# A gate matrix from one 256-column matmul a token, its two parts added on the way out of PSUM

## The chip, the cores and the metric

One core of a Trainium2 chip runs the whole program. The metric is the device time of one execution in microseconds (us); the median of several runs is compared. The profile comes from one execution of its own. Engines are named as the profile names them: PE is TensorE's matmul side and PEld its weight loads, DVE is VectorE, ACT is ScalarE, POOL is GpSimd, SP is SyncE, which issues most DMAs.

## What is computed

Two layers of a transformer-like backbone over 512 latent and 256 context tokens. Each layer ends in a PEER block: every token picks, for each of 8 heads, 16 of 16384 single-neuron experts by product keys, and sums gate times activation times value row. Cut to what matters here:

```python
best, ci = lax.top_k(cand, PEER_TOPK)            # 8 heads x 16 picks = 128 picks a token
i1 = take_along_axis(si[:, :, 0], ci // 16)      # first key index, 0..127
i2 = take_along_axis(si[:, :, 1], ci % 16)       # second key index, 0..127
expert = i1 * 128 + i2
gate = softmax(best)
act = gelu(einsum('td,thkd->thk', h, u[expert]))
out = einsum('thk,thkd->td', gate * act, v[expert])
```

For some 128-token tiles the kernel gathers the expert rows from HBM. For the others ("dense" tiles: all four latent tiles in layer 0, three in layer 1) it computes the activation of all 16384 experts and multiplies it by a matrix of gates that is zero outside the picks. That gate matrix is what the change touches.

## The kernel before

**The dense path.** The 16384 experts are 128 blocks `b` of 128. In the *scored* stage (`scored`, lines 1297 to 1325) each block's rows of u are loaded (`tab`, two blocks a DMA, from SP), cast to a high part on ACT (`uH`, line 1312), reduced to a low part on DVE (`uL`, line 1314), and multiplied with the tokens by 24 matmuls (`pa`, lines 133 to 135, 512 columns in layer 0, 384 in layer 1). ACT applies the gelu (`aw`, line 1318) and stores it to HBM, or keeps it in SBUF (`ar`) for the last blocks; a kept block is multiplied by its gates at once (line 1323). In the stage after it (`py`, lines 1348 to 1390) the stored activations are read back with the gates (`wt`, line 1360) and multiplied with the rows of v.

**The gates.** `gates` (lines 1202 to 1238) makes, for each token, the 128 x 128 matrix of gates over (i1, i2) by one-hots: with the picks on the partitions, `oh[:, 0]` is the one-hot of i1, `oh[:, 1]` that of i2 (both f16, from comparing `iota4` with the index, line 1226), and `og` (line 1229) is the first one-hot times the gate, twice: once with the f16 gate and once with what f16 rounding left of it. The product over the picks is a matmul. Four tokens go together (a *group*): two DVE instructions for the one-hots, one for `og`, 8 matmuls of 128 columns (line 1234: for each token the two parts accumulate in the same columns of PSUM), one ACT instruction (line 1235) that scales the four matrices and writes them into the tile `W`. The four tokens are the innermost, contiguous index of `oh` and `og`, so a matmul of one token reads its operands with a step of four f16 elements, 8 bytes, for the weights (`oh[:, 1, :, q]`) and for the moving columns alike. Eight groups fill `W` (2 MB), which a DMA from ACT's queue stores (line 1237). A tile has 32 groups: 128 in layer 0, 96 in layer 1, 224 in all, and 28 DMAs of `W`. `W` has one buffer; `pw` (PSUM), `oh` and `og` have two each.

**Order.** Every engine runs its own instructions in order. The order is made when the program is built, by a planner (`schedule_with_timeline_sim=True`, line 1562) that places instructions by priority and by durations of its own. `gated` is a generator: line 1338 draws its units between the blocks (a unit is the choice of the experts of a tile, or 8 groups), evenly over the first 19 (layer 0) or 15 (layer 1) sets of four blocks. When all are drawn, their SBUF is freed and used for kept activations (line 1344). Gathers for the other tiles run beside it: POOL issues them (line 1465), DVE takes the dot products and accumulates (lines 1476, 1483).

**PSUM.** The pool `pw` is opened at line 1295, before the scores (line 1328), with two buffers of one bank; the pools of the scores take three banks until they close, and `pa` and the modulation units have three.

Of the kernel before, what the change touches and what calls it, by code (L numbers as in the profile page):

```python
# [8 lines left out]
F32 = mybir.dt.float32  # L9
# [4 lines left out]
AF = mybir.ActivationFunctionType  # L14
OP = mybir.AluOpType
AX = mybir.AxisListType
PSUM = bass.MemoryType.PSUM

P = 128
# [10 lines left out]
GSCALE = 4096.0  # L30
# [36 lines left out]
class Kernel:  # L67
# [1134 lines left out]
    def gates(self, t, pk, pool, ps):  # L1202

        nc = self.nc
        pT = ps.tile([P, 3, P], F32, name="pT", tag="pw")
        for j in range(3):
            nc.tensor.transpose(pT[:, j], pk[:, j], self.ident)
        pkT = pool.tile([P, 3, P], F32, name="pkT")
        nc.scalar.copy(pkT, pT)

        gt = pool.tile([P, P], F32, name="gt")
        nc.vector.tensor_scalar(gt, pkT[:, 2], GSCALE, None, OP.mult)
        g2 = pool.tile([P, 2, P], F16, name="g2")
        nc.vector.tensor_copy(g2[:, 0], gt)
        nc.vector.tensor_tensor(g2[:, 1], gt, g2[:, 0], OP.subtract)
        ix = pool.tile([P, 2, P], F16, name="ix")
        nc.vector.tensor_copy(ix, pkT[:, 0:2])
        yield
        for s_ in range(4):
            W = pool.tile([P, P, 32], F32, name="W", bufs=1)  # L1220
            for t4 in range(8):
                tt = slice(s_ * 32 + t4 * 4, s_ * 32 + t4 * 4 + 4)

                oh = pool.tile([P, 2, P, 4], F16, name="oh")
                for z in range(2):
                    nc.vector.tensor_tensor(oh[:, z], self.iota4, ix[:, z, tt].unsqueeze(1).to_broadcast([P, P, 4]),  # L1226
                                            OP.is_equal)
                og = pool.tile([P, 2, P, 4], F16, name="og")
                nc.vector.tensor_tensor(og, oh[:, 0].unsqueeze(1).to_broadcast([P, 2, P, 4]),
                                        g2[:, :, tt].unsqueeze(2).to_broadcast([P, 2, P, 4]), OP.mult)  # L1230
                pw = ps.tile([P, 4, P], F32, name="pw")
                for q in range(4):
                    for z in range(2):
                        nc.tensor.matmul(pw[:, q], oh[:, 1, :, q], og[:, z, :, q], start=z == 0, stop=z == 1)  # L1234
                nc.scalar.activation(W[:, :, t4 * 4:t4 * 4 + 4], pw.rearrange("p q i -> p i q"), AF.Copy,  # L1235
                                     scale=1.0 / GSCALE)
            nc.scalar.dma_start(self.wscr[:, 4 * t + s_], W)
            yield

# [21 lines left out]
    def peer(self, l, st):  # L1261
        tc, nc, i = self.tc, self.nc, self.i
# [10 lines left out]
        with ExitStack() as sb:  # L1273
# [18 lines left out]
            if wc:  # L1292
                mu = (sb.enter_context(self.pool(name="mu", bufs=1)),
                      sb.enter_context(self.pool(name="psm", bufs=1, space=PSUM)))
            pw = sb.enter_context(self.pool(name="pw", bufs=2, space=PSUM))

            def scored(g, late=None):

# [27 lines left out]

            with ExitStack() as s2:
                self.scores(l, hH, hL, LAT, sv, sif, s2, gat.tick)
            if not wc:
                gat.pick(0, self.choose(3, sv, sif, sp, it), sp)  # L1330
            gp = sg.enter_context(self.pool(name="sg", bufs=2, side="right"))
# [235 lines left out]
```

## Time and profile before

| | |
|---|---|
| median of 3 runs | 4957.31 us (4954.19 to 4966.87) |
| the profiled execution | 4952.64 us; its span from first to last instruction 4950.8 us |
| PE busy | 4408.5 us, 89% of the span, 27525 matmuls |
| DVE busy | 3639.2 us, 74% |
| ACT busy | 1870.6 us, 38% |
| POOL busy | 1322.9 us, 27% |
| mean granted TensorE clock | 0.92 |

The page's first part gives busy time of each engine; its shares are averages over stages with different limits. So the stages with gates are read apart: layer 0 makes them from 1260 to 1880 us, layer 1 from 3760 to 4180 us. A window's row gives busy time and the number of instructions of each engine, the granted clock (1.00 is 2.4 GHz, 0.50 is 1.2 GHz), and what the DMA engines did. Matmuls are pipelined: the duration of one is longer than the distance to the next.

### The profile page before, as it was taken

The numbers are of one execution on the slowest core, as the hardware profiler recorded it, in microseconds if no ns is written. First come the engines' busy times: TensorE is split into PE (matmuls) and PEld (weight loads), VectorE is DVE, ScalarE is ACT, GpSimd is POOL, SyncE is SP. The second block draws the span as 40 slices with busy tenths as digits, with TensorE's granted clock in tenths as the row PEclk, the third lists the DMA queues.
The fourth block names the chain that finished last, engine by engine and source line by source line (L and its number), as shares of the span: only waits on it lengthen the run. The fifth ranks groups of instructions, "written<-read, shape, count | busy, mean of one in ns | idle before, by whom it ended". The sixth has DMA issues, their size and how long they took to land. (4 is left out here: it accounts for less than half of the span.)

```text
span 4950.8 us, 73840 instructions
## 1 busy us (share of the span) xinstructions
PE 4408.5 (89%) x27525; PEld 3651.6 (74%) x27525; DVE 3639.2 (74%) x7395; ACT 1870.6 (38%) x3349; POOL 1322.9 (27%) x1390
## 2 busy tenths in 40 slices
PE   7778797889999988999999887898898998999899
PEld 4567676677788777788777655876688897977787
DVE  3974666879976775788888787658489865779855
ACT  3533245433333333333333353345333333333333
POOL 0026641243211112332322133453123200223100
PEclk8778787899999989999999887888899998999999
DMA  7444655347887878999999644664428865899975
GB/s 270 151 115 115 180 164 173 108 162 280 291 312 272 326 274 302 354 333 368 366 353 356 215 131 107 172 189 129 141 77 306 327 226 189 309 338 355 349 220 182
DMA packets 544360, 1186.54 MB, mean 240 GB/s; under 512 B 62768, under 2 KB 342720, under 8 KB 491264
## 3 DMA queue, kind: packets, MB, share of 16 engines
q1 hardware_dynamic: 436624, 615.77, 37.8%
q0 software_dynamic: 72432, 460.62, 25.7%
q10 hardware_dynamic: 34944, 105.43, 5.6%
q8 instruction: 216, 3.54, 0.3%
q14 instruction: 144, 1.18, 0.1%
HBM read 1005.19 MB, written 176.50 MB: 239 GB/s over the span
## 5 line engine op out<-in xcount | busy, mean ns | idle before, releaser
L1465 POOL DMA_INDIRECT row<-in_uv,eidx x384 | 593.9, 1547 | 1529.4 <-DVE accc L1483 1125.7
L133 PE MATMUL pa<-hH,uH 128*128 128x512 f32 (+1 forms) x2048 | 760.7, 371 | 43.4 <-ACT aw L1318 28.1
L135 PE MATMUL pa<-hH,uL 128*128 128x512 f32 (+1 forms) x2048 | 760.0, 372 | 23.7 <-DVE uL L1314 23.5
L134 PE MATMUL pa<-hL,uH 128*128 128x512 f32 (+1 forms) x2048 | 753.8, 368 | 0.0
L134 PE MATMUL py<-vL,GH 128*128 128x512 f32 x1792 | 700.7, 393 | 11.8 <-DVE vL L1370 11.6
L135 PE MATMUL py<-vH,GL 128*128 128x512 f32 x1792 | 696.1, 390 | 0.0
L133 PE MATMUL py<-vH,GH 128*128 128x512 f32 x1792 | 589.8, 394 | 50.9 <-ACT vH L1368 41.9
L1476 DVE SCALAR_TENSOR_TENSOR row<-row,h2c 128x1024 f32<-128x1024 f32 x384 | 472.3, 1235 | 77.3 <-DMA row<-in_uv,eidx 76.6
L1483 DVE SCALAR_TENSOR_TENSOR accc<-row,dt,accc 128x1024 f32<-128x1024 f32 x384 | 497.7, 1296 | 36.8 <-ACT dt L1480 29.3
L1312 ACT CAST uH<-tab 128x1024 fp32r<-128x1024 f32 x256 | 268.7, 1050 | 657.9 <-PE pa L134 622.2
L133 PEld LDWEIGHTS pa<-hH,uH 128*128 128x128 f32 x2048 | 393.1, 192 | 92.6 <-ACT aw L1318 35.1
L135 PEld LDWEIGHTS pa<-hH,uL 128*128 128x128 f32 x2048 | 392.3, 192 | 80.3 <-DVE uL L1314 33.9
L133 PEld LDWEIGHTS py<-vH,GH 128*128 128x128 f32 x1792 | 336.4, 189 | 132.1 <-ACT vH L1368 53.3
L134 PEld LDWEIGHTS pa<-hL,uH 128*128 128x128 f32 x2048 | 392.4, 192 | 40.3 <-issue 0.4
L134 PEld LDWEIGHTS py<-vL,GH 128*128 128x128 f32 x1792 | 338.0, 189 | 95.3 <-DVE vL L1370 25.7
L1314 DVE TENSOR_TENSOR uL<-tab,uH 128x1024 fp32r<-128x1024 f32 x256 | 318.7, 1246 | 115.6 <-ACT uH L1312 115.3
L135 PEld LDWEIGHTS py<-vH,GL 128*128 128x128 f32 x1792 | 337.4, 188 | 69.8
L1370 DVE TENSOR_TENSOR vL<-tab,vH 128x1024 fp32r<-128x1024 f32 x256 | 308.6, 1220 | 18.2 <-ACT vH L1368 18.0
L1379 ACT CAST GH<-G 128x512 fp32r<-128x512 f32 (+1 forms) x180 | 102.9, 572 | 518.9 <-PE py L134 365.5
L1226 DVE TENSOR_TENSOR oh<-iota,ix 128x512 f16<-128x512 f16 x448 | 171.8, 423 | 144.1 <-PE pw L1234 144.0
L1234 PE MATMUL pw<-og,oh 128*128 128x128 f16 x1792 | 238.1, 297 | 41.8 <-ACT W L1235 25.3
L1368 ACT CAST vH<-tab 128x1024 fp32r<-128x1024 f32 x256 | 261.0, 1044 | 23.1 <-DMA tab<-in_uv 23.1
(382 smaller groups left out, 8595.5 us busy)
## 6 DMA issues: line engine op xcount, KB each, us to landing
tab<-in_uT SPq DMA_DIRECT2D x128, 1024.0 KB
tab<-in_uv SPq DMA_DIRECT2D x128, 1024.0 KB
wscr<-W ACTq DMA_DIRECT2D x28, 2048.0 KB
wmod<-in_w_mod SPq DMA_DIRECT2D x48, 512.0 KB
row<-in_wq SPq DMA_DIRECT2D x24, 1024.0 KB
ascr<-aw ACTq DMA_DIRECT2D x96, 256.0 KB
row<-in_w_mod POOLq DMA_DIRECT2D x24, 1024.0 KB
av<-ascr SPq DMA_DIRECT2D x48, 512.0 KB
```

Of the source, the lines that this page charges most:

```text
L133: mm(out, lh, rh, start=first, stop=False)
L134: mm(out, lh, rl, start=False, stop=False)
L135: mm(out, ll, rh, start=False, stop=last)
L1226: nc.vector.tensor_tensor(oh[:, z], self.iota4, ix[:, z, tt].unsqueeze(1).to_broadcast([P, P, 4]), OP.is_equal)
L1234: nc.tensor.matmul(pw[:, q], oh[:, 1, :, q], og[:, z, :, q], start=z == 0, stop=z == 1)
L1312: nc.scalar.copy(uH, ur)
L1314: nc.vector.tensor_tensor(uL, ur, uH.bitcast(F32), OP.subtract)
L1368: nc.scalar.copy(vH, vr)
L1370: nc.vector.tensor_tensor(vL, vr, vH.bitcast(F32), OP.subtract)
L1465: self.K.nc.gpsimd.indirect_dma_start(out=r, out_offset=None, in_=self.K.i[f"uv{self.l}"], in_offset=bass.IndirectOffsetOnAxis(ap=self.idx ...
L1476: nc.vector.scalar_tensor_tensor(rows[z][:, 0:D], rows[z][:, 0:D], 1.0, self.h[:, a], OP.mult, OP.mult, accum_out=dt[:, z:z + 1])
L1483: nc.vector.scalar_tensor_tensor(acc, v, dt[:, z:z + 1], acc, OP.mult, OP.add)
```

## The change

For each group of four tokens: the two one-hots are made by one DVE instruction; the two parts of `og` are read as one moving operand of 256 columns, so that a token has one matmul (4 a group, not 8) and its two parts land side by side in PSUM; ACT scales the first part into `W` as before, and a new DVE instruction adds the second part, scaled, to what ACT wrote. `pw` doubles to two banks a buffer, and its pool is opened after the scores.

```diff
-                for z in range(2):
-                    nc.vector.tensor_tensor(oh[:, z], self.iota4, ix[:, z, tt].unsqueeze(1).to_broadcast([P, P, 4]),
-                                            OP.is_equal)
+                nc.vector.tensor_tensor(oh, self.iota4.unsqueeze(1).to_broadcast([P, 2, P, 4]),
+                                        ix[:, :, tt].unsqueeze(2).to_broadcast([P, 2, P, 4]), OP.is_equal)
...
-                pw = ps.tile([P, 4, P], F32, name="pw")
+                pw = ps.tile([P, 4, 2, P], F32, name="pw")
                 for q in range(4):
-                    for z in range(2):
-                        nc.tensor.matmul(pw[:, q], oh[:, 1, :, q], og[:, z, :, q], start=z == 0, stop=z == 1)
-                nc.scalar.activation(W[:, :, t4 * 4:t4 * 4 + 4], pw.rearrange("p q i -> p i q"), AF.Copy,
-                                     scale=1.0 / GSCALE)
+                    nc.tensor.matmul(pw[:, q], oh[:, 1, :, q], og[:, :, :, q], start=True, stop=True)
+                w4 = W[:, :, t4 * 4:t4 * 4 + 4]
+                nc.scalar.activation(w4, pw[:, :, 0].rearrange("p q i -> p i q"), AF.Copy, scale=1.0 / GSCALE)
+                nc.vector.scalar_tensor_tensor(w4, pw[:, :, 1].rearrange("p q i -> p i q"), 1.0 / GSCALE, w4, OP.mult,
+                                               OP.add)
             nc.scalar.dma_start(self.wscr[:, 4 * t + s_], W)
...
-            pw = sb.enter_context(self.pool(name="pw", bufs=2, space=PSUM))
...
                 self.scores(l, hH, hL, LAT, sv, sif, s2, gat.tick)
+            pw = sb.enter_context(self.pool(name="pw", bufs=2, space=PSUM))
```

## Rows read from the trace of the kernel before

**Rows 1.** The page's first part: busy us, share of the span, instructions.
```profile
PE 4408.5 (89%) x27525; PEld 3651.6 (74%) x27525; DVE 3639.2 (74%) x7395; ACT 1870.6 (38%) x3349; POOL 1322.9 (27%) x1390
```
**Rows 2.** Windows: length, busy PE, PEld, DVE, ACT, POOL (instructions), clock, DMA.
```profile
1260.00:1440.00 180.00, 177.91 (x909) 142.99 (x908) 159.37 (x341) 67.30 (x117) 40.53 (x27) 0.98 0.84 304
1440.00:1830.00 390.00, 381.86 (x2067) 309.44 (x2065) 278.25 (x448) 142.47 (x259) 67.72 (x51) 0.99 0.81 298
3640.00:3780.00 140.00, 129.46 (x708) 123.41 (x707) 134.11 (x521) 55.12 (x85) 28.00 (x32) 0.98 0.58 209
3780.00:4000.00 220.00, 195.97 (x1164) 184.83 (x1164) 190.35 (x314) 85.78 (x163) 63.97 (x32) 0.95 0.85 312
4000.00:4150.00 150.00, 145.86 (x937) 140.96 (x937) 87.67 (x153) 59.08 (x91) 0.00 (x0) 0.99 0.55 194
```
**Rows 3.** Windows of tile pw alone: length, busy PE, ACT (instructions), clock, DMA.
```profile
1260.00:1440.00 180.00, 27.27 (x208) 14.36 (x25) 0.98 0.84 304
1440.00:1830.00 390.00, 88.52 (x672) 49.61 (x86) 0.99 0.81 298
1830.00:1882.00 52.00, 19.63 (x144) 11.01 (x19) 0.54 0.45 170
3780.00:4000.00 220.00, 45.41 (x336) 24.48 (x42) 0.95 0.85 312
4000.00:4150.00 150.00, 42.04 (x320) 22.49 (x39) 0.99 0.55 194
4150.00:4178.00 28.00, 15.23 (x112) 9.36 (x16) 0.50 0.34 138
```
**Rows 4.** Groups by line: count, busy us, mean ns, idle before and its releaser.
```profile
L1226 DVE TENSOR_TENSOR oh<-iota,ix 128x512 f16<-128x512 f16 x448 | 171.8, 423 | 144.1 <-PE pw L1234 144.0
L1229 DVE TENSOR_TENSOR og<-oh,g 128x1024 f16<-128x1024 f16 x224 | 152.4, 689 | 0.0
L1234 PE MATMUL pw<-og,oh 128*128 128x128 f16 x1792 | 238.1, 297 | 41.8 <-ACT W L1235 25.3 <-DVE og L1229 16.0 <-issue 0.5
L1235 ACT ACTIVATE W<-pw 128x512 f32<-128x512 f32 x224 | 131.3, 596 | 195.7 <-PE pw L1234 155.0 <-DMA wscr<-W 36.7 <-ACT aw L1318 0.9
```
**Rows 5.** Timeline (start us, us, what, count): full clock, half clock, half-clock `pa`.
```profile
1501.77 1.11 PE L1234 MATMUL pw<-og,oh 128*128 128x128 f16 x8
...
1832.62 1.11 PE L1234 MATMUL pw<-og,oh 128*128 128x128 f16 x8 [2.80 <-DVE og L1229]
...
1876.53 0.63 PE L135 MATMUL pa<-hH,uL 128*128 128x512 f32 x1
1876.95 0.63 PE L133 MATMUL pa<-hH,uH 128*128 128x512 f32 x1
```
**Rows 6.** Windows around the first two of Rows 5: columns as in Rows 2.
```profile
1501.00:1503.00 2.00, 2.00 (x15) 1.56 (x13) 0.09 (x1) 1.26 (x2) 0.00 (x0) 1.00 0.98 401
1832.50:1835.00 2.50, 1.11 (x8) 0.83 (x8) 2.50 (x6) 0.81 (x3) 0.00 (x0) 0.50 0.97 390
```
**Rows 7.** Timeline: the burst's first weight load, and its first two merged.
```profile
1501.76 0.11 PEld L1234 LDWEIGHTS <-oh 128*128 128x128 f16 x1 [0.26 <-issue]
...
1501.76 0.15 PEld L1234 LDWEIGHTS <-oh 128*128 128x128 f16 x2 [0.26 <-issue]
```
**Rows 8.** Timeline: successive matmuls of 256 contiguous columns, each with its own weights.
```profile
852.97 0.28 PE L135 MATMUL pq<-cH,wL 128*128 128x256 f32 x1
...
853.09 0.28 PE L133 MATMUL pq<-cH,wH 128*128 128x256 f32 x1
```
**Rows 9.** Groups by line and shape: DVE's scalar-tensor-tensor of some 512 elements.
```profile
L303 DVE SCALAR_TENSOR_TENSOR raw<-pf,colp,raw 128x511 f32<-128x511 f32 x30 | 22.3, 743 | 36.7 <-ACT raw L302 36.7
...
L810 DVE SCALAR_TENSOR_TENSOR aT<-kkT,aT 128x512 f32<-128x512 f32 x24 | 31.7, 1322 | 19.6 <-ACT kd L807 18.3 <-issue 0.9 <-POOL PLt L849 0.2
```
**Rows 10.** Chain that ended last, layer 1's last gates: start us, us, what.
```profile
4154.88 0.60 DVE og L1229
4155.48 0.67 DVE oh L1226 x2
...
4161.16 6.26 DMA wscr<-W
```

## The prediction

> **What bounds the kernel now.** I read the page's busy shares first, then windows over the two stretches that make gates, then the groups by line, and last the timeline of single bursts and the chain that ended last. PE leads with 89%, DVE follows with 74% [rows 1]; no instruction outside the gates changes, so only their stretches count. There I see two regimes. In the first, PE is the bound: it is busy 178 of 180 us, 382 of 390 and 146 of 150, while DVE has room in the second and the last of these (71% and 58%) and little in the first (89%). Layer 1's opening, 3780 to 4000, is tight on both: PE 89%, DVE 87% [rows 2]. DVE's waits say that its room is real: before line 1226 it idled 144 us, for PE to free a one-hot buffer [rows 4]. The second regime is each layer's last groups, where the score matmuls have run out: 18 groups (144 of 8 matmuls) in a window where pw's matmuls are 20 of 52 us, and 14 groups in 28 us [rows 3]. There the chain goes through DVE, two one-hots 0.67 us and `og` 0.60 us a group, and through the DMA of `W`, 6.3 us [rows 10]; kept activations wait behind it. So 192 groups lie beside PE's work and 32 in the open.
>
> **PE, removed: four matmuls and four weight loads a group.** A burst of 8 takes 1.11 us with a mean of 297 ns each, so they start (1.11 - 0.297)/7 = 0.116 us apart [rows 4, 5]; a group holds PE for 8 x 0.116 = 0.93 us. The question is what sets 0.116. Three rows speak: it is the same 0.116 at a granted clock of 1.00 and of 0.50 [rows 5, 6], where ordinary matmuls follow the clock (0.42 us apart for 512 columns at the half clock). A weight load is not it: one ends 0.11 us after it starts, two end 0.15 us after the first starts, so a second costs 0.04 [rows 7]. And one of these 128-column matmuls lasts 297 ns, longer than 256 contiguous columns, 280 ns [rows 4, 8]. So I take the columns themselves, read with a step of 8 bytes, to arrive at about 0.9 ns each whatever the clock. Then 256 of them cost nearly what two times 128 did. Bounds for the new distance: 0.12 us (256 contiguous columns with a weight load each [rows 8]) to 2 x 0.116 = 0.233; I take 0.22, near the upper end, allowing a little for the turn between matmuls that is saved. A group then takes 0.88 us, 0.05 less. Of the 192 covered groups the 84 + 40 in the PE-bound windows count [rows 3]: -6 us.
>
> The Trainium skill (TensorE: Matmul & The Clock Gate, § Back-to-back issue gap) puts the distance between warm matmuls at columns over 2.4 GHz plus 2.5 ns, an estimate of 109 ns for 256 columns, and 56 ns for 128, where the row shows 116. By that rule the group would drop from 0.93 to 0.44 us, which is the first rival below; the row for 128 columns already disagrees with it.
>
> **DVE, removed and added.** Two one-hot instructions held DVE 171.8/224 = 0.767 us a group; one of 1024 elements has the shape of `og`, 152.4/224 = 0.68 [rows 4]: -0.09. The new sum reads PSUM and `W` and writes `W`, 512 elements. Lower bound 0.743, the same operation out of PSUM; upper bound 1.32, the same operation out of SBUF where it was slowest [rows 9]. I take 0.743: it is also fed from PSUM, and ACT reads `pw` with such steps in 0.596 us [rows 4], no sign of a penalty. Net +0.656 us a group, 147 us of DVE work in all.
>
> The Trainium skill (Advanced Engine Details and Errata, § Memory Cachelines) says that PSUM has 8-byte lines and that two consecutive elements should be contiguous for best throughput. The sum steps over them; by that rule it would lie towards the upper bound, and no row here has DVE reading PSUM so.
>
> **Where that work falls.** DVE has been seen at 134/140 = 0.96 of a window [rows 2], so I count 0.95 as its ceiling. 1260 to 1440: 159.4 + 26 x 0.656 = 176.4, over 0.95 is 185.7, +6. 1440 to 1830: 278.3 + 84 x 0.656 = 333, 85% of 390, hidden under PE. 3780 to 4000: 190.4 + 42 x 0.656 = 217.9, over 0.95 is 229.4, +9. 4000 to 4150: 87.7 + 26.2 = 114 of 150, hidden. The cover is PE's own work; without it each group would cost its 0.656. The two tight windows border on loose ones into which the planner can push groups, so I take half of the 15: +8, and keep 0 and 15 as bounds.
>
> **The open groups.** On the chain a group now costs DVE 0.67 + 0.60 = 1.27 us [rows 10]; with the change 0.60 + 0.60 + 0.66 (the sum, less the 0.08 by which following DVE instructions overlap, 0.68 against 0.60) = 1.86, +0.59. 32 groups: +19 us. From below +15: at both ends of a `W` the chain runs through PE and ACT, and there the sum adds its 0.743 once before the DMA and once before the next burst, so a `W` costs 4 x 0.59 + 2 x 0.743, four times. From above +25: every group and both ends.
>
> **The new waits.** The sum waits for ACT, and DVE stands: behind it are `uL` of the next block, the next one-hots, the gathers' dot products. In the covered groups that is paid from DVE's room; if not, it shows as PE waiting for `uL` or `og`. The DMA of `W` now waits for the sum, and ACT's queue stands behind it with the casts `uH` and the gelus: 28 times some 0.74 us, 21 us, that I cost at nothing since ACT is 38% busy [rows 1]; exposed ones are in the +19. A `pw` buffer is freed by DVE, not ACT; two buffers stay. Opening the pool after the scores costs nothing: its first use needs the experts chosen from these scores. POOL's and SP's queues are passed by nothing.
>
> **Sum.** -6 + 8 + 19 = +21 us on the profiled execution's 4952.6, that is 4974 (1.8 us of it lie outside the span). The median stands 4.7 us above that execution, so 4957.3 + 21 = 4978 us. With the bounds, +9 to +34: 4966 to 4991.
>
> **Rivals.** *One weight load and 256 columns take 0.12 us* (faster). For it: contiguous columns do so [rows 8]. Against: clock-blind 0.116, 297 ns. A group falls to 0.48, -0.45. 1440 to 1830: 390 - 84 x 0.45 = 352, DVE needs 333/0.95 = 351: -38. 4000 to 4150: -18. Tight windows and open groups as above: +8 + 19. Together -29: 4928 us. It decides once a matmul starts less than about 0.17 us after the last, where PE's saving equals DVE's cost.
>
> *DVE becomes the bound* (slower by more). The sum is dear, or DVE's standing costs the covered groups. At 1.03 us, midway between the bounds, a group has +0.94. 1260 to 1440: 183.8/0.95 = 193.5, +13; 1440 to 1830: 357/0.95 = 376, hidden; 3780 to 4000: 229.8/0.95 = 242, +22; open groups 32 x 0.88 = +28; PE -6. Together +57: 5014 us. At 1.32 the same sum is +104. For it: 87 to 89% already in two windows; against: the PSUM row.
>
> *The planner's new order hides it* (no change). It lays all instructions anew, and the two open stretches of 80 us leave PE idle for more than half; an order that moves score matmuls into them takes back the 21. About 4957 us. Against: `W` has one buffer, its DMA of 6.3 us stays.
>
> **Chances.** Forecast 0.45, first rival 0.18, DVE the bound 0.22, new order 0.15. A measurement here can tell 0.3%, 15 us. Of the forecast two thirds lie above +15: slower 0.30, same 0.15. Slower: 0.30 + 0.22 + 0.02 = 0.54; same: 0.15 + 0.10 = 0.25; faster: 0.18 + 0.03 = 0.21. Range 4925 to 5030, which takes in both other signs and leaves out the dearest sums; the forecast's own is 4966 to 4991.
>
> **What would show it.** Line 1234 with 896 matmuls about 0.22 us apart and some 400 ns each, the same at half clock: the matmul step is right; 0.12: the first rival. One-hots at 0.69 us and the sum at 0.74: the DVE step. In the last groups of a layer a chain of DVE `oh`, `og`, `W` with 1.86 us a period: the open groups. PE waiting for `uL`, `og` or `W` in the covered windows, with DVE above 95%: DVE the bound. The prediction is wrong if PE's time in the gates halves, or if PE's idle time grows in windows where I gave DVE room.

## The result, and the profile after

The changed kernel takes 5029.6 us (median of 4 runs, 5028.9 to 5033.0) where the kernel before took 4955.8 beside it: ratio 1.0156, 95% interval 1.0133 to 1.0178. It is slower by 74 us; the forecast was 21 us. The profiled execution has a span of 5027.6 us against 4950.8, so 76.8 us are to be found in the traces.

The page's first part of after, as in [rows 1]: busy us, share of the span, instructions.

```profile
PE 4398.2 (87%) x26629; PEld 3552.8 (71%) x26629; DVE 3759.5 (75%) x7395; ACT 1868.0 (37%) x3345; POOL 1299.4 (26%) x1390
```

PE does 10 us less and DVE 120 us more, and yet neither share rose to a limit: PE fell from 89% to 87%, DVE stands at 75%. So no engine became the bound of the whole, and the time has to be looked for in waits. The groups by line of after, as in [rows 4] (count, busy us, mean ns, idle time before and its releaser):

```profile
L1233 PE MATMUL pw<-og,oh 128*128 128x256 f16 x896 | 235.0, 407 | 114.8 <-DVE og L1229 61.8 <-DVE W L1236 52.9
L1225 DVE TENSOR_TENSOR oh<-iota,ix 128x1024 f16<-128x1024 f16 x224 | 153.3, 690 | 88.3 <-PE pw L1233 88.1
L1229 DVE TENSOR_TENSOR og<-oh,g 128x1024 f16<-128x1024 f16 x224 | 152.0, 688 | 0.9
L1236 DVE SCALAR_TENSOR_TENSOR W<-pw,W 128x512 f32<-128x512 f32 x224 | 150.4, 687 | 42.3 <-ACT W L1235 42.2
L1235 ACT ACTIVATE W<-pw 128x512 f32<-128x512 f32 x224 | 130.9, 596 | 275.2 <-PE pw L1233 185.3 <-DMA wscr<-W 87.3 <-ACT aw L1318 1.2
```

The prices of single instructions are nearly those of the prediction: 407 ns for a matmul ("some 400"), 0.690 for the merged one-hots, 0.687 for the sum (0.743 was taken). What grew is the idle time: PE stood 114.8 us before line 1233, where it was 41.8 before line 1234 in before, and 52.9 of that are a new releaser, the sum that has to free a `pw` buffer. ACT's wait for the DMA of `W` went from 36.7 to 87.3.

Where PE stands is seen in the windows of after. The bounds are those of the two places where the score matmuls pause: they stop at 1794.0 and go on at 1915.3 us in layer 0, 4163.7 and 4258.3 in layer 1. In the kernel before the same two gaps were 1827.5 to 1874.2 and 4141.4 to 4183.2. First all instructions (columns as in [rows 2]), then those of tile `pw` alone (length, busy PE, DVE, ACT, clock, DMA, the counterpart of [rows 3]; four matmuls are one group now):

```profile
1278.00:1794.00 516.00, 509.21 (x2323) 379.09 (x2321) 413.66 (x640) 187.22 (x332) 87.92 (x70) 0.99 0.80 297
1794.00:1915.00 121.00, 47.28 (x181) 19.45 (x179) 96.49 (x153) 29.66 (x56) 3.97 (x3) 0.53 0.38 148
3828.00:4163.00 335.00, 312.19 (x1659) 277.09 (x1658) 271.73 (x388) 130.73 (x229) 42.30 (x31) 0.98 0.74 272
4163.00:4258.00 95.00, 39.99 (x153) 16.55 (x151) 68.62 (x113) 22.80 (x39) 0.00 (x0) 0.53 0.29 122
```

```profile
1278.00:1794.00 516.00, 86.78 (x336) 55.80 (x84) 48.92 (x84) 0.99 0.80 297
1794.00:1915.00 121.00, 46.43 (x176) 29.71 (x44) 25.73 (x44) 0.53 0.38 148
3828.00:4163.00 335.00, 63.69 (x240) 39.39 (x59) 35.16 (x60) 0.98 0.74 272
4163.00:4258.00 95.00, 38.08 (x144) 25.48 (x38) 21.07 (x36) 0.53 0.29 122
```

Line 1233 by window, for layer 0's covered stretch and its gap:

```profile
L1233 PE MATMUL pw<-og,oh 128*128 128x256 f16 x336 | 86.8, 407 | 0.0
...
L1233 PE MATMUL pw<-og,oh 128*128 128x256 f16 x176 | 46.4, 407 | 65.7 <-DVE og L1229 35.3 <-DVE W L1236 30.4
```

PE's waits for the sum all lie in the pauses, 30.4 us here and 22.5 in layer 1's; beside the score matmuls there is none.

176 matmuls of `pw` in the first gap are 44 groups, 144 in the second are 36: 80 open groups. The forecast was made with 32, and the program of before has 38 there (20 and 18: [rows 3] with its somewhat later bounds shows 18 and 14). The two gaps grew by 121.3 + 94.6 - 46.7 - 41.8 = 127 us. Outside them the span became 51 us shorter: 42 groups less to do beside the score matmuls, at 0.93 us of PE each 39 us, and some 12 us whose cause stays open.

What a group costs in a gap stands in the timeline of after (start us, us, engine, line, operation):

```profile
1849.33 0.69 DVE L1229 TENSOR_TENSOR og<-oh,g 128x1024 f16<-128x1024 f16 x1
...
1864.32 0.68 DVE L1236 SCALAR_TENSOR_TENSOR W<-pw,W 128x512 f32<-128x512 f32 x1
1864.92 0.68 DVE L1229 TENSOR_TENSOR og<-oh,g 128x1024 f16<-128x1024 f16 x1
1864.98 0.60 ACT L1235 ACTIVATE W<-pw 128x512 f32<-128x512 f32 x1 [1.20 <-PE pw L1233]
1865.52 0.69 DVE L1225 TENSOR_TENSOR oh<-iota,ix 128x1024 f16<-128x1024 f16 x1
1865.66 0.58 PEld L1233 LDWEIGHTS <-oh 128*128 128x128 f16 x4 [1.22 <-DVE og L1229]
1865.66 1.09 PE L1233 MATMUL pw<-og,oh 128*128 128x256 f16 x4 [0.72 <-DVE og L1229]
1866.13 0.68 DVE L1236 SCALAR_TENSOR_TENSOR W<-pw,W 128x512 f32<-128x512 f32 x1
...
1868.53 0.68 DVE L1229 TENSOR_TENSOR og<-oh,g 128x1024 f16<-128x1024 f16 x1
```

DVE runs without a break through sum, `og`, one-hots; one sum starts 1.81 us after the last (1864.32, 1866.13). The chain was 1.27 us a group before [rows 10], so an open group has become 0.54 dearer where the prediction had 0.59. From one `W`'s first `og` to the next `W`'s (1849.33, 1868.53) it is 19.2 us for 8 groups, 2.4 us each, with the DMA of `W` in it. So the price of an open group was nearly right, and their number was not: 38 x 0.54 = 21 us, 42 x 2.4 = 101 us, together 122 of the 127. In before the same two places stand 14.0 us apart in layer 0's gap:

```profile
1836.81 0.69 DVE L1229 TENSOR_TENSOR og<-oh,g 128x1024 f16<-128x1024 f16 x1
...
1850.81 0.69 DVE L1229 TENSOR_TENSOR og<-oh,g 128x1024 f16<-128x1024 f16 x1
```

With the ends of a `W` an open group thus became 0.65 us dearer, which makes it 25 + 101 = 126 us.

### The profile page after: what moved, and what is told of

Read it like the earlier page. It is cut to its first block, busy times and chain, and to the rows that moved or that the text cites. A ratio compares the mean times of both kernels' runs of the same rounds, so it can differ in the third digit from the quotient of the medians.

```text
span 5027.6 us, 71991 instructions
## 1 busy us (share of the span) xinstructions
PE 4398.2 (87%) x26629; PEld 3552.8 (71%) x26629; DVE 3759.5 (75%) x7395; ACT 1868.0 (37%) x3345; POOL 1299.4 (26%) x1390
## 4 chain that ended last, share of the span: by engine, by line
PE 54%; DVE 16%; DMA 12%; issue 9%; POOL 4%; ACT 4%; SPq 1%; ACTq 0%; DVEq 0%; POOLq 0%
PE py L134 9%; PE py L133 8%; PE py L135 8%; PE pa L135 4%; PE pa L133 4%; PE pa L134 4%; DMA row<-in_uv,eidx 3%; PE pw L1233 2%; PE pf L133 2%; PE pf L134 2%; PE pf L135 1%; DMA wscr<-W 1%; DVE accc L1484 1%; PE pg L841 1%; POOL row L1466 1%
## 5 line engine op out<-in xcount | busy, mean ns | idle before, releaser
L1466 POOL DMA_INDIRECT row<-in_uv,eidx x384 | 567.6, 1478 | 1553.7 <-DVE accc L1484 1170.0
L135 PE MATMUL pa<-hH,uL 128*128 128x512 f32 (+1 forms) x2048 | 762.1, 373 | 27.1 <-DVE uL L1314 26.7
L1477 DVE SCALAR_TENSOR_TENSOR row<-row,h2c 128x1024 f32<-128x1024 f32 x384 | 471.8, 1234 | 78.9 <-DMA row<-in_uv,eidx 71.8
L1233 PE MATMUL pw<-og,oh 128*128 128x256 f16 x896 | 235.0, 407 | 114.8 <-DVE og L1229 61.8
L1382 DVE TENSOR_TENSOR GL<-G,GH 128x512 fp32r<-128x512 f32 (+1 forms) x180 | 113.1, 629 | 197.9 <-ACT GH L1380 197.7
```

Source lines behind the costliest of these rows:

```text
L135: mm(out, ll, rh, start=False, stop=last)
L1233: nc.tensor.matmul(pw[:, q], oh[:, 1, :, q], og[:, :, :, q], start=True, stop=True)
L1382: nc.vector.tensor_tensor(GL, G, GH.bitcast(F32), OP.subtract)
L1466: self.K.nc.gpsimd.indirect_dma_start(out=r, out_offset=None, in_=self.K.i[f"uv{self.l}"], in_offset=bass.IndirectOffsetOnAxis(ap=self.idx ...
L1477: nc.vector.scalar_tensor_tensor(rows[z][:, 0:D], rows[z][:, 0:D], 1.0, self.h[:, a], OP.mult, OP.mult, accum_out=dt[:, z:z + 1])
```

## The experiments

How many groups stand behind the last score matmuls is no accident of a run. Every engine takes its instructions in the program's order, and that order is fixed when the kernel is built; it can be counted there: layer 0 stops its score matmuls after 98 blocks (layer 1 after 86) until all gates are made, because the kept activations need the gates' memory. Groups behind that place in PE's order (the "last early block" of the expectations) are open. The traces show the same places and the same counts in every run of the table. What the runs had to settle was which part of the change pushed them there, and why.

Theory A: the added DVE sum. Rival B: the wide matmul and its two-bank `pw`. Later, within A: A1, DVE has no time left beside the score matmuls; A2, the sum only makes a group hold its buffers (`oh`, `og`, `pw`, two each) for longer. Ratios are against runs of the kernel before on the same chip (medians 4950.2 to 4955.8); "open" is the count in the program's order, layer 0 + layer 1; "gaps" are the two pauses of the score matmuls in the trace.

| kernel | median us | ratio, 95% interval | open | gaps us |
|---|---|---|---|---|
| before | 4955.8 | 1 | 20 + 18 | 46.7, 41.8 |
| after | 5029.6 | 1.0156 [1.0133, 1.0178] | 44 + 36 | 121.3, 94.7 |
| e1_onehot | 4934.6 | 0.9969 [0.9951, 0.9986] | 22 + 14 | 48.7, 33.1 |
| e2_nosum | 4940.7 | 0.9971 [0.9956, 0.9986] | 20 + 14 | 45.4, 33.4 |
| e3_sum_alone | 5034.2 | 1.0156 [1.0133, 1.0178] | 42 + 34 | 118.1, 91.6 |
| e4_psum | 4950.5 | 1.0000 [0.9981, 1.0018] | 20 + 18 | 46.7, 41.8 |
| e5_deep | 4952.6 | 1.0003 [0.9986, 1.0019] | 20 + 12 | 64.1, 24.6 |
| e6_half | 4999.9 | 1.0116 [1.0095, 1.0137] | 38 + 32 | 96.2, 79.3 |
| e9_onehot_deep | 4899.9 | 0.9911 [0.9893, 0.9930] | 0 + 0 | none |
| e11_before_deep | 4892.9 | 0.9883 [0.9863, 0.9904] | 0 + 0 | none |
| e12_pw4 | 4980.6 | 1.0049 [1.0032, 1.0067] | 34 + 24 | 93.1, 57.3 |
| e13_after_oh3 | 5011.2 | 1.0125 [1.0096, 1.0155] | 38 + 30 | 103.5, 70.0 |

### e1_onehot: the merged one-hots alone

```diff
-                for z in range(2):
-                    nc.vector.tensor_tensor(oh[:, z], self.iota4, ix[:, z, tt].unsqueeze(1).to_broadcast([P, P, 4]),
-                                            OP.is_equal)
+                nc.vector.tensor_tensor(oh, self.iota4.unsqueeze(1).to_broadcast([P, 2, P, 4]),
+                                        ix[:, :, tt].unsqueeze(2).to_broadcast([P, 2, P, 4]), OP.is_equal)
```

> The kernel before with one part of the change alone: both one-hots in one DVE instruction. Theory A (the added DVE sum slows the groups, so that more of them are left when the score matmuls stop at blocks 98 and 214): no sum here, so the gaps in the score matmuls stay near 47 and 42 us or shrink by a few us, DVE has some 20 us less to do; 4940 to 4957 us. Rival B (the wide matmul or the two-bank PSUM tile slows the groups): the same, neither is here. If this kernel is slower than 4970 us, the merged one-hots are part of the loss and both theories lack something.

Measured: 4934.6, ratio 0.9969, 5 us below the expected band. The merged one-hots are a small gain by themselves; the loss is not theirs.

### e2_nosum: the change without its sum

```diff
-                nc.vector.scalar_tensor_tensor(w4, pw[:, :, 1].rearrange("p q i -> p i q"), 1.0 / GSCALE, w4, OP.mult,
-                                               OP.add)
```

> The changed kernel without the DVE sum: the second part of the gate (what f16 rounding left) is computed by the matmul and not added into W. Theory A: the gaps in the score matmuls fall back from 121 and 95 us to about 47 and 42 us, DVE has 154 us less to do (224 x 0.685); 4940 to 4960 us. Rival B (wide matmul, two-bank PSUM tile): the gaps stay near 121 and 95 us, about 5030 us.

Measured: 4940.7, ratio 0.9971, gaps 45.4 and 33.4 us. The wide matmul is there, with its 407 ns and some 0.23 us from start to start, and gives and costs nothing beyond e1. The whole loss hangs on the one DVE instruction.

### e3_sum_alone: the sum alone, on the kernel before

```diff
-                nc.scalar.activation(W[:, :, t4 * 4:t4 * 4 + 4], pw.rearrange("p q i -> p i q"), AF.Copy,
-                                     scale=1.0 / GSCALE)
+                w4 = W[:, :, t4 * 4:t4 * 4 + 4]
+                nc.scalar.activation(w4, pw.rearrange("p q i -> p i q"), AF.Copy, scale=1.0 / GSCALE)
+                nc.vector.scalar_tensor_tensor(w4, pw.rearrange("p q i -> p i q"), 0.0, w4, OP.mult, OP.add)
```

> The kernel before, its 8 matmuls of 128 columns, one-bank PSUM tile and two one-hot instructions, with a DVE sum of the changed kernel's size added after ACT: pw times zero added to W. Theory A: the gaps grow to 121 and 95 us or a little more, since DVE also keeps the second one-hot instruction; 5025 to 5050 us. Rival B: the sum is hidden beside PE but for the open groups, 4965 to 4980 us.

Measured: 5034.2, the same ratio as the whole change, with gaps of 118.1 and 91.6 us. Theory A stands.

### e4_psum: the two-bank pw, opened after the scores

```diff
-            pw = sb.enter_context(self.pool(name="pw", bufs=2, space=PSUM))
...
-                pw = ps.tile([P, 4, P], F32, name="pw")
+                pw = ps.tile([P, 4, 2, P], F32, name="pw")
...
                 self.scores(l, hH, hL, LAT, sv, sif, s2, gat.tick)
+            pw = sb.enter_context(self.pool(name="pw", bufs=2, space=PSUM))
```

> The kernel before with the PSUM part of the change alone: pw takes two banks a buffer (half of them unused) and its pool is opened after the scores. Theory A: nothing, 4945 to 4967 us. Rival B in its PSUM form: the gaps grow, over 4990 us.

Measured: 4950.5, ratio 1.0000, gaps unchanged. Rival B falls with e2 and e4.

### e5_deep: the sum alone, with more buffers (the "third experiment" is e3)

On the kernel of e3:

```diff
-                oh = pool.tile([P, 2, P, 4], F16, name="oh")
+                oh = pool.tile([P, 2, P, 4], F16, name="oh", bufs=3)
...
-                og = pool.tile([P, 2, P, 4], F16, name="og")
+                og = pool.tile([P, 2, P, 4], F16, name="og", bufs=3)
...
-            pw = sb.enter_context(self.pool(name="pw", bufs=2, space=PSUM))
...
+            pw = sb.enter_context(self.pool(name="pw", bufs=4, space=PSUM))
```

> The kernel of the third experiment (before, with the DVE sum of 512 elements out of PSUM after each eviction, one-bank pw), with more buffers for the gates: four pw instead of two, three oh and three og instead of two. DVE has the same instructions as there. Theory A2, buffers held longer: the sum made the groups slow because oh, og and pw come free later, so the order has 42 and 34 groups behind the last early block; with more buffers the order of this program has 20 and 12 there, the gaps in the score matmuls fall from 118 and 92 us to some 57 and 36, the 44 groups that are covered again cost PE 41 us, total about 4950 to 4965 us though DVE's added 0.68 us a group are all there. Theory A1, DVE's time itself: in the covered stretch DVE has no more time to give than it had, so the chip runs the earlier groups late and PE waits for them there instead; total stays within 10 us of 5034.

Measured: 4952.6, 82 us below e3 with the same DVE instructions. Windows of e5: first all instructions in the two covered stretches (columns as in [rows 2]), then tile `pw` alone in the covered stretch and the gap of each layer (length, busy PE, DVE, ACT, clock, DMA).

```profile
1280.00:1818.00 538.00, 530.78 (x2849) 431.30 (x2848) 456.66 (x814) 195.48 (x350) 100.28 (x69) 0.99 0.79 290
...
3787.00:4163.00 376.00, 348.74 (x2116) 331.12 (x2114) 326.40 (x555) 143.04 (x255) 47.06 (x31) 0.95 0.72 261
```

```profile
1280.00:1818.00 538.00, 112.33 (x863) 68.16 (x104) 59.09 (x104) 0.99 0.79 290
1818.00:1882.00 64.00, 21.24 (x160) 15.80 (x24) 13.38 (x24) 0.52 0.54 221
3787.00:4163.00 376.00, 89.41 (x672) 54.76 (x84) 47.35 (x84) 0.95 0.72 261
4163.00:4187.00 24.00, 12.57 (x96) 8.24 (x13) 6.85 (x12) 0.62 0.34 131
```

863 and 672 matmuls are 108 and 84 groups beside the score matmuls, each with its sum, where after has 84 and 60. DVE takes it: it is busy 85% and 87% of these stretches, while PE stays at 99% and 93%. After stood at 80% and 81% there. So DVE on the chip had the time, and A1 falls as it was put: with more buffers the order places 44 groups more beside the score matmuls, and DVE does them. That leaves 32 groups open; e11 below shows how many there are with the same buffers and no sum.

### e6_half: a sum over half of the columns

```diff
...
+                wh = W[:, 0:64, t4 * 4:t4 * 4 + 4]
+                nc.vector.scalar_tensor_tensor(wh, pw[:, :, 0:64].rearrange("p q i -> p i q"), 0.0, wh, OP.mult, OP.add)
```

> Before, with a DVE sum over half of the 512 columns (256 elements, about 0.37 us by the 0.685 for 512): the dose. The program's order has 38 and 32 groups behind the last early block (before 20 and 18, the full sum 42 and 34). If what counts is the number of groups left open, the time follows this number and not DVE's time: some 4.5 fifths of the groups for half of the sum; gaps of about 95 and 78 us, total about 5010 us. If the cost were in proportion to the DVE time added, half of the 79 us of the full sum: about 4995 us, gaps about 82 and 67.

Measured: 4999.9, gaps 96.2 and 79.3 us. The gaps are those that the count of open groups gave (95 and 78, not 82 and 67): half of the sum leaves 70 groups open, nearly as many as the whole one with 76. But half of the columns is more than half of the time:

```profile
L1238 DVE SCALAR_TENSOR_TENSOR W<-pw,W 128x256 f32<-128x256 f32 x224 | 89.9, 418 | 40.5 <-ACT W L1236 35.9 <-issue 3.9
```

418 ns of the 685 that the whole sum takes in e3 are 0.61, and in proportion to that the gaps would be 90 and 72 us. They still lie nearer to the count. The total decides nothing: by the medians it is 48 us above before, 0.61 of the whole sum's 79, and by the ratios 0.74 of it, with an interval that reaches down to 0.61.

### e8_contig: moving columns side by side

```diff
-                og = pool.tile([P, 2, P, 4], F16, name="og")
-                nc.vector.tensor_tensor(og, oh[:, 0].unsqueeze(1).to_broadcast([P, 2, P, 4]),
-                                        g2[:, :, tt].unsqueeze(2).to_broadcast([P, 2, P, 4]), OP.mult)
+                og = pool.tile([P, 4, 2, P], F16, name="og")
+                for z in range(2):
+                    nc.vector.tensor_tensor(og[:, :, z].rearrange("p q i -> p i q"), oh[:, 0],
+                                            g2[:, z:z + 1, tt].to_broadcast([P, P, 4]), OP.mult)
...
-                    nc.tensor.matmul(pw[:, q], oh[:, 1, :, q], og[:, :, :, q], start=True, stop=True)
+                    nc.tensor.matmul(pw[:, q], oh[:, 1, :, q], og[:, q], start=True, stop=True)
```

> After, with og laid token by token, so that a matmul's 256 moving columns lie side by side (the weights oh keep their step of 8 bytes); DVE writes og with a step, in two instructions, dearer than before. If the columns' step sets the pace (as the prediction took it), the matmuls of a burst start about 0.12 us apart instead of 0.230. If the stepped weights or the turn between matmuls set it, they stay near 0.23. The total is not the point: the order has 54 and 41 groups behind the last early blocks, some 5080 us or more.

Measured: one run of 5729.7 us, since DVE's `og` became very dear (below). The question was the matmul. Two bursts of four in the timeline of e8, and windows around them (the last three numbers are clock, DMA share, GB/s):

```profile
1300.75 0.63 PE L1234 MATMUL pw<-og,oh 128*128 128x256 f16 x4 [2.66 <-DVE og L1230]
...
1305.50 1.04 PE L1234 MATMUL pw<-og,oh 128*128 128x256 f16 x4 [3.56 <-DVE og L1230]
```

```profile
1300.70:1301.30 0.60, 0.55 (x4) 0.36 (x4) 0.60 (x3) 0.00 (x0) 0.00 (x0) 1.00 0.87 273
1305.50:1306.50 1.00, 1.00 (x8) 0.47 (x9) 1.00 (x2) 0.00 (x0) 0.00 (x0) 0.50 0.93 393
```

At a granted clock of 1.00 (2.4 GHz) such a matmul lasts 273 ns, so four start (0.63 - 0.273)/3 = 0.12 us apart; at 0.50 it lasts 417 ns and they start (1.04 - 0.417)/3 = 0.21 apart. With a step of 8 bytes between the columns after shows this, again at either clock:

```profile
1308.90 2.01 PE L1233 MATMUL pw<-og,oh 128*128 128x256 f16 x8
...
1858.97 1.99 PE L1233 MATMUL pw<-og,oh 128*128 128x256 f16 x8 [6.01 <-DVE W L1236]
```

```profile
1308.90:1310.90 2.00, 2.00 (x12) 0.91 (x10) 1.32 (x3) 1.01 (x2) 1.33 (x2) 1.00 0.94 385
1858.97:1860.97 2.00, 1.99 (x8) 0.86 (x7) 1.43 (x3) 0.60 (x1) 0.00 (x0) 0.50 0.00 0
```

(2.01 - 0.407)/7 = 0.229 at the full clock, and 0.226 in the gap, at a granted clock of 0.50. The weights kept their step in e8, so it is the moving columns' step that costs the kernel its 0.9 ns a column.

### e9_onehot_deep: e1 with more buffers (the "first experiment" is e1)

Besides the edit of e1:

```diff
-                oh = pool.tile([P, 2, P, 4], F16, name="oh")
+                oh = pool.tile([P, 2, P, 4], F16, name="oh", bufs=3)
...
-                og = pool.tile([P, 2, P, 4], F16, name="og")
+                og = pool.tile([P, 2, P, 4], F16, name="og", bufs=3)
...
-            pw = sb.enter_context(self.pool(name="pw", bufs=2, space=PSUM))
...
+            pw = sb.enter_context(self.pool(name="pw", bufs=4, space=PSUM))
```

> Before with the merged one-hots (first experiment) and deeper buffers: four pw, three oh, three og. The program's order has no group behind the last early block (22 and 14 with two buffers each). Theory A2, buffers: the two gaps of 49 and 33 us in the score matmuls go almost wholly, 36 groups more are covered at 0.93 us of PE each, total about 4935 - 82 + 33 = 4886 us, 4875 to 4900. Theory A1, DVE's time is what limits the groups beside the score matmuls: PE waits for DVE earlier instead, and the total stays at 4925 to 4940.

Measured: 4899.9, ratio 0.9911; the score matmuls have no gap left. Faster than both kernels.

### e11_before_deep: nothing but the buffers (the "ninth experiment" is e9)

On the kernel before, and nothing else:

```diff
-                oh = pool.tile([P, 2, P, 4], F16, name="oh")
+                oh = pool.tile([P, 2, P, 4], F16, name="oh", bufs=3)
...
-                og = pool.tile([P, 2, P, 4], F16, name="og")
+                og = pool.tile([P, 2, P, 4], F16, name="og", bufs=3)
...
-            pw = sb.enter_context(self.pool(name="pw", bufs=2, space=PSUM))
...
+            pw = sb.enter_context(self.pool(name="pw", bufs=4, space=PSUM))
```

> Before with nothing but more buffers for the gates: four pw, three oh, three og (pw opened after the scores). The program's order has no group behind the last early block, where before has 20 and 18. Theory A2, buffers alone decide: the gaps of 47 and 42 us in the score matmuls go, 38 more groups are covered at 0.93 us of PE each, total about 4952 - 53 = 4900 us (4890 to 4915). If instead the shorter one-hots were what made the ninth experiment fast, the total stays at 4930 to 4950.

Measured: 4892.9, ratio 0.9883: 57 us faster than before with no instruction changed. In its windows of tile `pw` (length, busy PE, ACT, clock) all 1024 + 768 matmuls lie in the covered stretches:

```profile
1272.00:1785.00 513.00, 131.25 (x1024) 71.94 (x127) 1.00 0.82 301
3756.00:4100.00 344.00, 100.81 (x768) 53.62 (x96) 0.98 0.76 281
```

So the kernel before was already held by these buffers. The merged one-hots add nothing to it: e9 has 4899.9, and the intervals of the two ratios overlap. And with the buffers given, the sum still costs 4952.6 - 4892.9 = 60 us (e5 against e11): its order keeps 32 open groups where there are none without it. With two buffers each it costs 5034.2 - 4954.9 = 79 us (e3 against before on its chip), 38 open groups. So the buffers weigh on the kernel with the sum and without it, and A2 explains little of what the sum itself costs: only some 20 of its 79 us go away with more buffers, about as much as the intervals leave open. Why the order leaves so many groups open when the sum is there, these runs don't show.

### e12_pw4: the sum alone, with four pw only

On the kernel of e3:

```diff
-            pw = sb.enter_context(self.pool(name="pw", bufs=2, space=PSUM))
...
+            pw = sb.enter_context(self.pool(name="pw", bufs=4, space=PSUM))
```

> The kernel of the third experiment (before, with the DVE sum) with four pw instead of two, and oh and og at two as before: which buffer is the short one? The program's order has 34 and 24 groups behind the last early block (42 and 34 with two pw, 20 and 12 with everything deeper). By 2.4 us an open group and 0.93 us a covered one: gaps of about 97 and 68 us, total about 5034 - 45 + 17 = 5006 us. If pw alone were the short one, about 4955; if oh and og alone, about 5034.

Measured: 4980.6, gaps 93.1 and 57.3 us: 54 of the 82 us that e5 gave. So `pw` is the larger part of the shortage and not all of it; the sum with more `oh` and `og` alone was not run on this kernel. The total is 25 us below what I worked out from the count. The gaps, 15 us shorter than expected, are the larger part; the other 10 us are the distance from the median to the profiled run, which at 4991.1 is the longest of nine.

### e13_after_oh3: the change, with three oh and og

On the changed kernel:

```diff
-                oh = pool.tile([P, 2, P, 4], F16, name="oh")
+                oh = pool.tile([P, 2, P, 4], F16, name="oh", bufs=3)
...
-                og = pool.tile([P, 2, P, 4], F16, name="og")
+                og = pool.tile([P, 2, P, 4], F16, name="og", bufs=3)
```

> The changed kernel with three oh and three og (PSUM has no room for four pw of two banks). The program's order has 38 and 30 groups behind the last early block instead of 44 and 36. By 2.4 us an open group and 0.92 us a covered one: gaps of about 110 and 85 us, total about 5030 - 29 + 11 = 5012 us. If oh and og were what the sum holds up, about 4960.

Measured: 5011.2, as expected for the count of open groups, but in part by luck: the gaps are 103.5 and 70.0 us, 21 us less in all than the 110 and 85 from which the total was worked out. Three `oh` and `og` give 18 us on the changed kernel; four `pw`, which gave 54 us on the kernel of e3 with one bank each, were not run with the two banks of the change.

### e10_rows: the columns side by side, made row by row

```diff
-                oh = pool.tile([P, 2, P, 4], F16, name="oh")
...
+                oh = pool.tile([P, P, 4], F16, name="oh", bufs=3)
+                nc.vector.tensor_tensor(oh, self.iota4, ix[:, tt].unsqueeze(1).to_broadcast([P, P, 4]), OP.is_equal)
+                og = pool.tile([P, 4, 2, P], F16, name="og", bufs=3)
+                for q in range(4):
+                    for z in range(2):
+                        c = s_ * 32 + t4 * 4 + q
+                        nc.vector.tensor_scalar(og[:, q, z], self.iota1, pkT[:, 0, c:c + 1], gf[:, z, c:c + 1],
+                                                OP.is_equal, OP.mult)
...
-                        nc.tensor.matmul(pw[:, q], oh[:, 1, :, q], og[:, z, :, q], start=z == 0, stop=z == 1)
+                        nc.tensor.matmul(pw[:, q], oh[:, :, q], og[:, q, z], start=z == 0, stop=z == 1)
...
-            pw = sb.enter_context(self.pool(name="pw", bufs=2, space=PSUM))
...
+            pw = sb.enter_context(self.pool(name="pw", bufs=4, space=PSUM))
```

> Before with four pw, and og laid token by token (128 columns side by side for each part), made straight from the indices by eight instructions of 128 elements a group (compare with the index, times the gate) in place of the first one-hot and og; the second one-hot stays one instruction of 512. PE: if the columns' step sets a matmul's pace, the eight start 0.06 us apart instead of 0.118, and a group holds PE for some 0.48 us less. DVE: 0.42 + 8 x t against 1.45 us now; t is open, 0.225 us being the length of the nearest row (128 elements, f32 to f32) and 0.1 about a half of it. With t near 0.12: no change on DVE, total about 4900 - 100 = 4800 us. With t near 0.22: DVE has +0.73 us a group, 164 us in all, and becomes the bound beside the score matmuls: 4860 to 4950 us.

Measured: 5134.5, ratio 1.0372 [1.0350, 1.0394], slower than either number. PE's part came out as expected where a group's operands are ready: a burst of eight takes 0.64 us instead of 1.11, its matmuls 0.06 us apart, at a granted clock of 1.00 (the burst in the timeline, then a window around it, columns as in [rows 2]):

```profile
1322.99 0.64 PE L1239 MATMUL pw<-og,oh 128*128 128x128 f16 x8
...
1322.90:1323.50 0.60, 0.60 (x11) 0.51 (x10) 0.00 (x0) 0.60 (x2) 0.00 (x0) 1.00 0.87 321
```

But the small instructions cost what the dear case said. A group by line (count, busy, mean ns) and three of them in a row in the timeline:

```profile
L1234 DVE TENSOR_SCALAR og<-iota,pkT,gf 128x128 f16<-128x128 f16 x1792 | 427.1, 308 | 0.1
```

```profile
1503.45 0.74 DVE L1234 TENSOR_SCALAR og<-iota,pkT,gf 128x128 f16<-128x128 f16 x3
```

(0.74 - 0.308)/2 = 0.22 us each, 1.7 for eight. The order of this program bunches groups early (16, 24 and 13 in a row after blocks 30, 38 and 44 of layer 0; 30 and 20 in layer 1), and there the score matmuls pause for 51.6, 78.7, 48.8, 112.9 and 53.0 us, with DVE busy all the time: in the window of the longest,

```profile
3908.00:4021.00 113.00, 57.33 (x249) 25.61 (x248) 113.00 (x336) 24.69 (x61) 25.08 (x20) 0.51 0.67 244
```

113 of 113 us. Here DVE is the bound, which it was not in after. Why the order bunches them so stays open.

## Why the prediction was wrong, point by point

**What bounds the kernel.** The two regimes were right. Wrong was the reading of one row: "DVE's waits say that its room is real: before line 1226 it idled 144 us, for PE to free a one-hot buffer" [rows 4]. The row says that DVE had time, which e5 confirms, but it says as well that a group can't start while its buffers are held, and their number helped to set how many groups fit beside the score matmuls of before. e11 shows it by its time: more buffers, the same instructions, no open group, 57 us less. The row itself would not have told: DVE's wait for PE before line 1226 fell from 144.0 us to 71.6 in e11, the fastest kernel, and to 74.2 in e3, which is slower than before.

```profile
L1226 DVE TENSOR_TENSOR oh<-iota,ix 128x512 f16<-128x512 f16 x448 | 167.3, 419 | 72.0 <-PE pw L1234 71.6
...
L1226 DVE TENSOR_TENSOR oh<-iota,ix 128x512 f16<-128x512 f16 x448 | 170.5, 421 | 74.3 <-PE pw L1234 74.2
```

**PE.** Right in its mechanism: 0.9 ns a column, whatever the clock; 0.23 us where 0.22 was taken. The saving is thus 8 x 0.116 - 4 x 0.23 = 0.01 us a group, not 0.05, and the -6 us are about -1. The first rival (0.12 us) is dead as long as the columns keep their step, and e8 shows that it would hold without it. The Trainium skill (TensorE: Matmul & The Clock Gate, § Back-to-back issue gap) gives the formula that the prediction used for an isolated matmul, and for a stream of weight loads and matmuls, which this is, about 81 ns at 128 columns. By the formula 256 columns are an estimate of 109 ns; e8 with contiguous columns agrees at the full clock (0.12), and after with its step does not (0.229). At 128 columns e10's contiguous ones, 0.06 us apart, lie at the formula's 56 ns and not at 81, and before's stepped ones, 0.116, at neither.

**DVE's prices.** One-hots 0.690, `og` 0.688, the sum 0.687: +0.6 us a group, within a tenth of the forecast. The sum reads PSUM with a step and shows no penalty next to the 743 ns of [rows 9]. The rule of the Trainium skill (Advanced Engine Details and Errata, § Memory Cachelines), that two consecutive elements should lie side by side in PSUM, is not borne out by that row.

**The tight windows**, +8 us. This term was of the wrong kind. In the same stretches of after (columns as in [rows 2]; layer 1's gates begin 48 us later there, at 3828.8 instead of 3780.5, so the second window is moved by that),

```profile
1260.00:1440.00 180.00, 179.25 (x827) 135.44 (x826) 166.01 (x327) 69.70 (x120) 31.90 (x25) 1.00 0.81 294
...
3828.00:4048.00 220.00, 197.19 (x1034) 174.50 (x1033) 195.93 (x287) 85.94 (x162) 42.30 (x31) 0.97 0.85 314
```

DVE is busy 92% and 89%, under the 0.95 that I took for its ceiling. Of tile `pw` alone these windows hold 96 and 136 matmuls, 24 and 34 groups at four each, where before had 208 and 336 at eight, 26 and 42 [rows 3]. The order did push groups out of these windows, as the prediction allowed, but not into the loose ones: the covered stretches hold 144 groups in all where before had 186, and the rest went into the open end.

**The open groups**, +19 us. This is the step that failed. "192 groups lie beside PE's work and 32 in the open" was read from before and then kept as a constant of the kernel. The price of 0.59 a group was nearly right (0.54). But their number is an outcome of the order, and the order of before ended in open groups already. With the sum in the loop of every group it left more of them: 38 became 80 in after, 76 with the sum alone (e3), and 34 without the sum (e2). With that number and the measured prices the term becomes 38 x 0.54 = 21 and 42 x (2.4 - 0.93) = 62, together +83 for a measured +77 of the span.

**The new waits.** "A `pw` buffer is freed by DVE, not ACT; two buffers stay" names a possible part of the cause in passing and gives it no price. On the chip it shows as PE's 52.9 us before line 1233 with the sum as releaser, all of it in the two gaps and so within the price of the open groups. Beside it stands the order, which was made with such a loop in it; four `pw` instead of two took 54 us off the kernel with the sum alone (e12), and what they alone give without the sum was not run. ACT stood 87.3 us for the DMA of `W` instead of 36.7, but mostly because more groups are open: in the gaps it is 61.5 us for 80 groups, in before 27.1 for 38, some 0.7 to 0.8 a group both times.

**The rivals.** DVE as the bound gives a time near the measured one, 5014, by another mechanism: it wants DVE above 95% in the covered windows, and over these stretches it is at 80%. That the stated range of 4925 to 5030 just takes in 5029.6 is owed to this rival's sum and is luck. Nor did PE's idle time grow where DVE was given room, the sign that the prediction named: beside the score matmuls PE is busy 99% and 93% in after, 98% and 93% in before. The new order was on the list, but only as something that could hide the cost. That it could also make it larger, the same mechanism with the other sign, was not.

What stays open is why the builder, with the sum in the loop, leaves more groups behind the score matmuls. Its own reckoning was seen only through the order that came out, and no run took the order of before with the sums put into it. The hold of `oh`, `og` and `pw` is at most a small part (e5 against e11: the sum costs 60 us with more of them, 79 without). For the rest two rivals stand untested: that DVE is full in the builder's reckoning though not on the chip, and the one buffer of `W`, which the sum holds longer and which no run made two.

## What to carry to other kernels

Where work hides beside a bound engine, count how much of it fits before the cover ends, and ask what sets that number; if a tail already sticks out, a step added to the loop can put whole pieces into the tail, at the open price less the hidden one, not only its own duration. A wait on a buffer's release in a stretch where the waiting engine has time can mean that depth, not work, is short. The length of the wait doesn't say so, a run with more buffers does: here it gave 57 us with no instruction changed. And moving a sum out of the accumulating matmul into the eviction puts one more step, and one more engine, into the loop of every piece: here one instruction of 0.69 us a group, on an engine with room beside the score matmuls, cost 79 us by itself (e3).

## What the runs showed of the hardware

A matmul that reads its moving f16 columns with a step of 8 bytes takes 0.9 ns a column at both levels of the granted clock (0.229 and 0.226 us for 256 columns in after), while contiguous ones follow the clock (0.12 and 0.21 us in e8, whose weights keep the step). DVE pays for a step on the writing side: `og` of 512 elements, written in e8 with 512 bytes between neighbours, took 2.58 us, where 1024 elements side by side take 0.69.

```profile
L1230 DVE TENSOR_TENSOR og<-oh,g 128x512 f16<-128x512 f16 x448 | 1063.2, 2579 | 0.7
```

And 128 elements a piece is small for DVE: 0.22 us each (e10), so that eight pieces cost 1.7 us where one instruction of 1024 elements, of another operation, costs 0.69.
